# First row block of V computed transposed, with 512 tokens moving past tiles of the weights

## The chip and the metric

The kernel runs on one core of a Trainium2 chip. The metric is device time in microseconds, the median of several runs. The profile is one execution recorded by the hardware profiler; its times are microseconds from the span's start. The engines are PE (TensorE, matmuls; PEld its weight loads), DVE (VectorE), ACT (ScalarE), POOL (GpSimd) and SP (SyncE, which issues nearly all DMAs here).

## The reference

One encoder block on 1024 tokens of width 1024: a joint projection, two groups of attention heads, gates, an output projection and a layer norm.

```python
h = x @ W_in                     # q, k, v, gate of group a; q, k, v, gate of group b
# group a: 8 heads of 64, 2-D neighbourhood attention (8 x 16 window) with a relative bias
# group b: 8 query heads on 2 key/value heads, |i - j| <= 128, rotary positions, a sink logit
p = softmax(q k^T * scale + bias or mask);  o = p v
y = concat(o_a * silu(gate_a), o_b * silu(gate_b)) @ W_out
out = layer_norm(alpha * x + y)
```

The values (V) of both groups are 640 of the columns of `h`: 512 of group a and 128 of group b. The host lays x out transposed (`xT`, columns of x as partitions) and hands the 640 columns apart as `wv`, 1024 x 640.

## The kernel before

The kernel is one function, `hybrid_block`, called by `kernel`. The order of every engine's work is that of the code (`tc.manual_schedule()`, L664), with a list of events that are run at given counts of projection matmuls.

Every product of two f32 matrices is made in three passes from high and low parts: high x high, low x high, high x low. TensorE multiplies a stationary operand of 128 columns, which a weight load brings in, with a moving one.

**Values, first block.** The 1024 tokens are two row blocks of 512. The scales with which x and wv become f16 need the maximum of all x and the sums of wv, so they are not known while the data still arrive. The first block is therefore made in F32R, with parts of x (`xh`, `xl`) and of wv (`wvh`, `wvl`) cast by ACT and subtracted by DVE (POOL for the last two k). First come 26 spins on a small tile (`warm`, L492). `first_tiles` (L528) brings in the first k (128 rows of xT and wv) in halves of 256 tokens and 320 columns; later k's come whole (`load_x`, `load_wv`). `v_mms` (L556) then makes, for each k, four tiles of 128 tokens x two halves of 320 columns x three passes: the stationary operand is 128 tokens of x, the moving one 320 columns of wv, 24 matmuls a k and 192 in all. The sums stand in eight PSUM banks (`tags`, L662).

**Values, second block.** `scales()` (L690) makes `runit` and the like. ACT makes the f16 high parts, DVE the low ones (`x16_part`, `wv_hi`, `wv_lo`), and `v_mms` runs 192 f16 matmuls of 320 columns (L714 on) for the tokens 512 to 1023. Meanwhile `v_out` (L652) copies the first block's banks to `v32[t]`, six by ACT and two by DVE, and `v_max` (L659) takes the maxima of V.

**The projections and what runs beside them.** Then come six projections of 48 f16 matmuls of 512 columns (`project`, L440; the matmul is L459). `at(c, fn)` (L804) hangs a function on matmul c, and these are the ones of this case:

- `v_scale` (L764) at 16: the maximum over the partitions through a transposition on TensorE (L767) and DVE's chain to `vrs`, the reciprocal scale of V.
- the rotary tables cos and sin (`table_load`, L758) at 20.
- `v_part(t)` (L777) at 30 + 8t, one for each of eight token tiles: ACT makes the f16 high part `vt` (L790), DVE the low part (L780) and the copy of group b's part into `vb` (L781), and SP two stores of group a's part to DRAM (`vd`, L783), from where it is fetched row by row later.
- `sum_w(i)` (L793) and `w_scan` take the absolute sums of weight columns on ACT (L799, L270) and DVE (L801). `w_scale(m)` adds them up over the partitions with a tiny matmul on TensorE (L276); DVE's chain L277 to L281 makes the scale `wsc`. With it ACT makes the weights' f16 high part (`wh`, L250) and POOL the low part (`wl`, L255 and L256). A weight buffer (`wr`, L239, two for each projection tile, counted wr0, wr1, ...) is loaded anew when POOL is through with it. In the trace the tiny matmuls of `w_scale(2)` to `w_scale(5)` stand before 68.88, 79.26, 89.65 and 100.03 us, and the last one (`w_scale(NPRO)`) before 106.75.

SP's queue is in order: a DMA whose condition isn't met holds up those behind it. The other engines' queues are in order too.

**Attention.** The unit loop from L1609 on runs heads and row tiles: scores, softmax (`stage_exp`), DMA transposes of the probabilities from `split` to `tr` (L972), products with V (`stage_pv`, L998, which takes `vb` for group b). POOL clears the six `split` tiles beforehand (L857 to L860). The output projection and the norm follow.

Of the kernel before, what the change touches and what calls it, by code (L numbers as in the profile page):

```python
# [7 lines left out]
F32 = mybir.dt.float32  # L8
# [62 lines left out]
def hybrid_block(ctx, tc, xT, x, wt, wv, wo, bias, sink, gain, lbias, cos, sin, bmask, out):  # L71
# [413 lines left out]
    with ExitStack() as vctx:  # L485
# [4 lines left out]
        ps = bank("t")  # L490
        for _ in range(26):
            nc.tensor.matmul(ps[:, :128], warm, warm, start=True, stop=True)  # L492
# [35 lines left out]
        def first_tiles():  # L528
            xr = vp.tile([128, 512], F32, tag="xr", name="xraw", bufs=4)
            wr = wv_stage(0)  # L530
            h = vw.tile([128, 640], F32R, tag="wvh0", name="wvh0")
            l = vw.tile([128, 640], F32R, tag="wvl0", name="wvl0")
            wvh.append(h)
            wvl.append(l)
            for a in (0, 256):
                if a == 0:
                    nc.sync.dma_start(wr[:, :320], wv[0, :, :320])
                nc.sync.dma_start(xr[:, a:a + 256], xT[0, 0, :, a:a + 256])
            nc.sync.dma_start(wr[:, 320:], wv[0, :, 320:])
            xa, xb = xh[0, 0], xl[0, 0]  # L540
            for a in range(2):
                xs, ws = slice(256 * a, 256 * a + 256), slice(320 * a, 320 * a + 320)
                nc.scalar.copy(h[:, ws], wr[:, ws])
                nc.vector.tensor_copy(xa[:, xs], xr[:, xs])
                nc.vector.tensor_sub(xb[:, xs], xr[:, xs], xa[:, xs].bitcast(F32))
                nc.vector.tensor_sub(l[:, ws], wr[:, ws], h[:, ws].bitcast(F32))

# [8 lines left out]
        def v_mms(ps, t, a, k, passes=(0, 1, 2)):  # L556
            ts = slice(128 * (t % 4), 128 * (t % 4) + 128)
            cs = slice(320 * a, 320 * a + 320)
            for i in passes:
                if t < 4:  # L560
                    lh, rh = ((xh[0, k], wvh[k]), (xl[0, k], wvh[k]), (xh[0, k], wvl[k]))[i]
                else:
                    (xa, xb), (wa, wb) = (x16h[1, k], x16l[1, k]), wv16[k]
                    lh, rh = ((xa, wa), (xb, wa), (xa, wb))[i]
                ko = KO if t >= 4 else range(KT)
                nc.tensor.matmul(ps[:, :320], lh[:, ts], rh[:, cs],  # L566
                                 start=(k == ko[0] and i == 0), stop=(k == ko[-1] and i == 2))

# [39 lines left out]
        def wv_hi(k):  # L608
            nc.scalar.activation(wv16[k][0], wraw[k], AF.Copy, scale=wvs)
# [38 lines left out]

        v32 = [vw.tile([128, 640], F32, name=f"v32_{t}") for t in range(8)]
        vm = vw.tile([128, 8], F32, name="vm")  # L650

        def v_out(ps, t, a, eng="act"):  # L652
            cs = slice(320 * a, 320 * a + 320)
            if t >= 4:
                nc.scalar.activation(v32[t][:, cs], ps[:, :320], AF.Copy, scale=vdq)
            else:
                (nc.scalar.copy if eng == "act" else nc.vector.tensor_copy)(v32[t][:, cs], ps[:, :320])

        def v_max(t):  # L659
            nc.vector.tensor_reduce(vm[:, t:t + 1], v32[t], axis=AXX, op=ALU.max, apply_absolute_value=True)  # L660

        tags = ("pj", "pj", "s", "s", "t", "t", "s", "s")  # L662
        banks = [bank(t) for t in tags]
        ordered.enter_context(tc.manual_schedule())  # L664
        first_tiles()
        interleave(load_x(0, 1), load_wv(1))
        for k in range(KT):
# [12 lines left out]
            if k < 5 or k == 6:  # L680
                interleave(*gens)
            for a in range(2):
# [20 lines left out]

        wv_hi(KO[0])
        x16_part(1, KO[0])
        for i, eng in ((0, "act"), (2, "act"), (6, "dve"), (1, "dve"), (3, "act"), (7, "act")):
            v_out(banks[i], i // 2, i % 2, eng)
        wv_lo(KO[0])
        ahead(1)
        v_out(banks[4], 2, 0)  # L710
        ahead(2)
        v_out(banks[5], 2, 1)
        nc.vector.tensor_mul(vdq, unit[:, 0:1], unit[:, 1:2])
# [8 lines left out]
        for i, k in enumerate(KO):  # L722
# [10 lines left out]
            if i in (4, 6):  # L733
                w_scale(i // 2 - 2)
            if i >= 4:
                v_max(i - 4)
        for t in (0, 1, 3):
# [3 lines left out]
        for a in range(2):  # L741
            ps = bank(tags[4 + a])
            for k in KO:
                v_mms(ps, 6, a, k)
            if a == 0:
                x16_part(0, 1)
                w_split(0)
                x16_part(0, 2)
                v_max(4)
            else:  # L750
                x16_part(0, 3)
                v_max(5)
                v_max(7)
                w_split(1)
            v_out(ps, 6, a)
        v_max(6)

# [19 lines left out]
        def v_part(t):  # L777
            if t > 0:
                vt, v3 = vts.pop(t - 1)
                nc.vector.scalar_tensor_tensor(vt[:, :, 1, :HD], v3, vrs, vt[:, :, 0, :HD], op0=ALU.mult, op1=ALU.subtract)  # L780
                nc.vector.tensor_copy(vb[:, t - 1], vt[:, 8:10, :, :HD])  # L781
                for i in range(2):
                    nc.sync.dma_start(  # L783
                        vd[:, :, 2 * (t - 1) + i, :].rearrange("q c e -> c q e"),
                        vt[GW * i:GW * i + GW, 0:8].rearrange("p (q h) i e -> p q (h i e)", h=2))
            if t < 8:
                vt = vp.tile([128, 10, 2, VE], F16, tag=("vt", "wvr")[t % 2], name=f"vt{t}", bufs=3)
                v3 = v32[t].rearrange("p (h e) -> p h e", e=HD)
                nc.gpsimd.memset(vt[:, 0:8, :, HD:VE], 1.0 / PSCALE)
                nc.scalar.activation(vt[:, :, 0, :HD], v3, AF.Copy, scale=vrs)  # L790
                vts[t] = vt, v3

# [186 lines left out]
    def stage_pv(q):  # L979
        ps = st[q, "o"] = bank("t")  # L980
        for m in range(4):
# [6 lines left out]
            for i in range(c):  # L988
# [4 lines left out]
                else:  # L993
                    v = [vb[d, k, p // 2, e, :] for e in range(2)]
                ph, pl = tr[d, i, :], tr[d, c + i, :]
# [788 lines left out]
```

## Time and profile before

| | |
|---|---|
| median of 3 runs | 432.82 us (432.66 to 433.52) |
| the profiled execution | 433.62 us, span 431.7 us, granted clock 0.999 |
| spins | 0.99 to 3.94 us |
| first k of the values; second k on | 3.87 to 8.6 us; from 8.64 us |
| f16 block of the values | from 33.39 us |
| projections | from 59.70 us |
| PE busy in each ten us from 10 to 130 | 10.00 |

The first half of a row of the page names the line, the engine, the operation and the tiles written and read; then come count, busy time and mean length of one, and the idle time of the engine just before, with what ended it. Matmuls overlap, so the pitch of a row of them is read from their starts, not from their lengths.

### The profile page before, as it was taken

The page shows a single profiled execution, that of the slowest core. Times are in us where ns is not written, and L with a number is a line of the kernel's source. Part 1 is how long each engine was busy: PE and PEld are TensorE (multiplying, and loading weights), DVE is VectorE, ACT ScalarE, POOL GpSimd, SP SyncE. Part 2 cuts the span into 40 slices and gives each one's busy share as a digit, 9 for nine tenths or more (in the row PEclk, how much of TensorE's full clock was granted, in tenths as well). Part 3 has the DMA queues.
Part 4 walks back from the last instruction along what each step waited for, and adds up shares of the span by engine and source line. Part 5 has one row for each costly group of instructions (what it writes and reads, how often), then busy time and mean ns, then how long its engine had stood idle before and what let it go on. Part 6 is the DMA issues. An engine that isn't in the chain of part 4 may idle for free.

```text
span 431.7 us, 9375 instructions
## 1 busy us (share of the span) xinstructions
PE 425.5 (99%) x3175; PEld 249.1 (58%) x3175; DVE 343.5 (80%) x856; ACT 317.8 (74%) x682; POOL 291.4 (67%) x300
## 2 busy tenths in 40 slices
PE   8999999999999999999999999999999999999995
PEld 7997764444445555656555655555565655444444
DVE  4978966884887888888789897897887875597685
ACT  4759789888659989778998866889878883653313
POOL 0030075789468867788999977668889799649354
PEclk9999999999999999999999999999999999999999
DMA  7947768992448999989799999997999989942222
GB/s 249 392 167 241 240 197 291 278 318 55 140 135 173 192 167 219 197 157 154 146 225 229 199 171 187 246 178 125 237 194 200 187 169 234 402 172 97 99 98 99
DMA packets 131552, 84.81 MB, mean 196 GB/s; under 512 B 97584, under 2 KB 106928, under 8 KB 131504
## 3 DMA queue, kind: packets, MB, share of 16 engines
q1 hardware_dynamic: 131360, 84.08, 81.6%
q8 instruction: 25, 0.41, 0.4%
q14 instruction: 23, 0.19, 0.2%
q10 hardware_dynamic: 144, 0.13, 0.1%
HBM read 50.60 MB, written 10.52 MB: 142 GB/s over the span
## 4 chain that ended last, share of the span: by engine, by line
PE 94%; DMA 2%; POOL 1%; ACT 0%; SPq 0%; DVE 0%; issue 0%; POOLq 0%; ACTq 0%
PE ps_pj L459 50%; PE ps_t L998 7%; PE ps_s L1310 7%; PE ps_s L566 6%; PE ps_pj L1310 5%; PE ps_t L1310 4%; PE ps_s L921 4%; PE ps_s L922 4%; PE ps_pj L566 3%; PE ps_t L566 3%; PE ps_t L1035 2%; DMA wvraw<-in_wv 1%; DMA tr<-split 1%; POOL xr L1455 0%; POOL xr L1458 0%
## 5 line engine op out<-in xcount | busy, mean ns | idle before, releaser
L459 PE MATMUL ps_pj<-xf,wh 128*128 128x512 f16 x672 | 201.3, 379 | 0.0
L459 PE MATMUL ps_pj<-xf,wl 128*128 128x512 f16 x336 | 127.3, 379 | 0.0
L459 PEld LDWEIGHTS <-wh 128*128 128x128 f16 x672 | 63.7, 98 | 58.3
L951 ACT ACTIVATE ps_s<-sn,nm 128x321 f32<-128x321 f32 (+3 forms) x128 | 67.8, 529 | 32.0 <-DVE nm L935 30.4
L970 DVE SCALAR_TENSOR_TENSOR split<-ps_s,split 128x320 f16<-128x320 f32 (+2 forms) x128 | 62.6, 489 | 18.4 <-ACT split L969 16.8
L255 POOL TENSOR_SCALAR wr<-wr,wsc 128x512 f32<-128x512 f32 x32 | 23.9, 746 | 55.9 <-ACT wh L250 51.3
L969 ACT ACTIVATE split<-ps_s 128x320 f16<-128x320 f32 (+2 forms) x128 | 55.1, 430 | 3.1 <-DMA tr<-split 1.3
L459 PEld LDWEIGHTS <-wl 128*128 128x128 f16 x336 | 32.8, 98 | 37.9
L935 DVE CUSTOM_DVE_ANT_0 sn<-ps_s,bm,nsk 128x320 f32<-128x320 f32 (+2 forms) x64 | 37.0, 579 | 8.9 <-PE ps_s L922 8.7
L256 POOL TENSOR_TENSOR wl<-wr,wh 128x512 f16<-128x512 f32 x32 | 39.6, 1238 | 2.7
L935 DVE CUSTOM_DVE_ANT_0 sn<-ps_s,bias,sg 128x368 f32<-128x368 f32 (+1 forms) x64 | 36.1, 564 | 3.7 <-PE ps_s L922 3.3
L921 PE MATMUL ps_s<-ks,qs 128*128 128x320 f16 (+3 forms) x128 | 38.2, 298 | 0.0
L922 PE MATMUL ps_s<-ks,qs 128*128 128x320 f16 (+3 forms) x128 | 38.2, 298 | 0.0
L998 PEld LDWEIGHTS <-tr 128*128 128x128 f16 (+1 forms) x1056 | 36.3, 98 | 2.3 <-DMA tr<-split 0.4
L369 POOL COPY ks<-ks 64x512 f16<-64x512 f16 x40 | 25.9, 647 | 8.4 <-ACT ks L313 6.0
L1310 PEld LDWEIGHTS <-m 128*128 128x128 f16 x186 | 17.8, 98 | 19.3 <-POOL m L1231 0.2
L1455 POOL TENSOR_TENSOR xr<-xr,gb 128x512 f32<-128x512 f32 (+1 forms) x11 | 12.3, 1123 | 18.3 <-ACT xr L1439 18.3
L250 ACT ACTIVATE wh<-wr,wsc 128x512 f16<-128x512 f32 x32 | 22.7, 710 | 0.9 <-DVE wsc L280 0.9
L566 PEld LDWEIGHTS <-xf 128*128 128x128 f16 x192 | 18.6, 98 | 7.3
L921 PEld LDWEIGHTS <-qs 128*128 128x128 f16 x128 | 12.5, 98 | 15.1
L922 PEld LDWEIGHTS <-qs 128*128 128x128 f16 x128 | 12.5, 98 | 15.0
L998 PE MATMUL ps_t<-va,tr 128*128 128x65 f16 (+1 forms) x528 | 19.1, 193 | 0.0
(269 smaller groups left out, 933.1 us busy)
## 6 DMA issues: line engine op xcount, KB each, us to landing
wr<-in_wt SPq DMA_DIRECT2D x32, 256.0 KB, 3.3
ws<-in_wt SPq DMA_DIRECT2D x15, 512.0 KB, 6.3
wor<-in_wo SPq DMA_DIRECT2D x20, 256.0 KB, 4.1
xr<-in_x SPq DMA_DIRECT2D x8, 512.0 KB, 9.7
out<-xr SPq DMA_DIRECT2D x14, 256.0 KB, 2.0
bias<-in_bias SPq DMA_DIRECT2D x8, 440.0 KB, 4.3
wob<-in_wo SPq DMA_DIRECT2D x12, 256.0 KB, 4.2
wvraw<-in_wv SPq DMA_DIRECT2D x9, 320.0 KB, 6.4
```

Source lines behind the costliest of these rows:

```text
L256: nc.gpsimd.tensor_sub(l, raw, h)
L369: nc.gpsimd.tensor_copy(place(t, o, half, col), place(t, a, half, col))
L459: nc.tensor.matmul(ps, a[:, k % 4, :], mv, start=(k == 0 and i == 0), stop=(k == KT - 1 and i == 2))
L566: nc.tensor.matmul(ps[:, :320], lh[:, ts], rh[:, cs], start=(k == ko[0] and i == 0), stop=(k == ko[-1] and i == 2))
L921: nc.tensor.matmul(ps[:, :n], q, sl[0], start=True, stop=False)
L922: nc.tensor.matmul(ps[:, :n], q, sl[1], start=False, stop=True)
L935: nc.vector.tensor_tensor_reduce(sn[:, at0:at0 + n], ps[:, :n], bias_t, sg[:, c:c + 1], init, op0=ALU.add, op1=ALU.min, accum_out=nm)
L951: nc.scalar.activation(pt[:, c], sn[:, c], AF.Exp, bias=nm, scale=-1.0, accum_out=acc)
L969: nc.scalar.activation(h, pt[:, c], AF.Copy, scale=PSCALE)
L970: nc.vector.scalar_tensor_tensor(l, pt[:, c], PSCALE, h, op0=ALU.mult, op1=ALU.subtract)
L998: nc.tensor.matmul(ps[:, w * m:w * m + e], a, b_, start=(i == 0), stop=(i == len(mms) - 1))
L1310: nc.tensor.matmul(ps[:, cs], lh[:, 128 * t:128 * t + 128], rh[:, cs], start=(fresh and e == 0 and n == 0), stop=(e == len(terms) - 1 and ...
```

## The change

The first block of V is made transposed: the stationary operand is now a tile of 128 columns of wv (five of them, `j`), the moving one all 512 tokens of x. `vt_mm` (L570 of the changed kernel) makes 15 matmuls of 512 columns a k, 120 in all, two of which are made in halves of 256; five banks hold the sums. The first k goes in an order of its own, k = 1 to 6 pass by pass, the last k bank by bank. Eight spins go, and two matmuls of 512 columns on `warm` (L671) clear the two banks into which halves are added. `first_tiles` cuts wv into 256 and 384 columns, and ACT casts the second half of x.

On PE, this is what stands where the second k of the first block begins (bank<-operands, columns). Before:

```order
L566 MATMUL ps_pj<-wvh_214,x_79 128x320
L566 MATMUL ps_s<-wvh_214,x_79 128x320
L566 MATMUL ps_t<-wvh_214,x_79 128x320
L566 MATMUL ps_s<-wvh_214,x_79 128x320
L566 MATMUL ps_pj<-wvh_214,x_79 128x320
L566 MATMUL ps_s<-wvh_214,x_79 128x320
```

And now, the whole of that k:

```order
L570 MATMUL ps_s<-x_79,wvh_206 128x512 x3
L570 MATMUL ps_t<-x_79,wvh_206 128x512 x2
L570 MATMUL ps_s<-x_79,wvh_206 128x512 x3
L570 MATMUL ps_t<-x_79,wvh_206 128x512 x2
L570 MATMUL ps_s<-x_79,wvl_207 128x512 x3
L570 MATMUL ps_t<-x_79,wvl_207 128x512 x2
```

The six rows before are a quarter of a k; the six now are all 15 matmuls of one.

The evacuation is five copies of 512 columns (`vt_out`, L662; DVE for j = 0, 1, 3, ACT for 2 and 4), and the maxima are taken of five tiles of 512 and four of 640. `v_scale` is hung on step 10, cos on 10 and sin on 12.

V of the first block must then be turned. For each j, `vt_part` (ACT, high part) and `vt_part2` (DVE, low part) fill `vhl`; `vt_turn` (L825) is a DMA transpose of eight blocks of 128 x 128, f16, for j = 4 straight into `vb`, for the others into `vtd`; `vt_store` (L830, L832) copies these on DVE into `vtt` with the columns of ones and stores them to `vd`. The token tiles 4 to 7 keep their way in `v_part` and `v_part2`. Each step hangs on 26 + 6.4 (n + step). The layout of `vb` changes with it, and `stage_pv` reads it accordingly.

This is SP's queue about the rotary tables. Before (`wr` weight loads, `ws` loads for the weight sums, `vd` the stores):

```order
L239 DMA wr_891<-in_wt 128x512
L239 DMA wr_912<-in_wt 128x512
L720 DMA ws_917<-in_wt 128x2x512
L760 DMA cos<-in_cos 128x1024
L760 DMA sin<-in_sin 128x1024
L720 DMA ws_952<-in_wt 128x2x512
L783 DMA vd<-vt_957 64x4x260 x2
L720 DMA ws_980<-in_wt 128x2x512
L783 DMA vd<-vt_972 64x4x260 x2
L239 DMA wr_1008<-in_wt 128x512
```

Now:

```order
L239 DMA wr_811<-in_wt 128x512
L776 DMA cos<-in_cos 128x1024
L776 DMA sin<-in_sin 128x1024
L239 DMA wr_845<-in_wt 128x512
L736 DMA ws_850<-in_wt 128x2x512
L736 DMA ws_874<-in_wt 128x2x512
L825 DMA_TRANSPOSE vb<-vhl_869 128x8x128
L736 DMA ws_903<-in_wt 128x2x512
L825 DMA_TRANSPOSE vtd_915<-vhl_882 128x8x128
L239 DMA wr_931<-in_wt 128x512
L825 DMA_TRANSPOSE vtd_937<-vhl_894 128x8x128
```

The tables stand one weight load and one `ws` load earlier, and transposes stand where stores stood; the stores follow later.

And this is DVE's queue ahead of the chain of `w_scale(3)` (`wg`). Before:

```order
L801 TENSOR_REDUCE wm<-ws_694 128x1
L780 SCALAR_TENSOR_TENSOR vt_1063<-v_5_179,vrs,vt_1063 128x10x64
L781 COPY vb<-vt_1063 128x256
L780 SCALAR_TENSOR_TENSOR vt_1086<-v_6_180,vrs,vt_1086 128x10x64
L781 COPY vb<-vt_1086 128x256
L277 TENSOR_REDUCE wg<-ps_t 128x1
```

Now:

```order
L842 TENSOR_REDUCE wm<-ws_614 128x1
L830 COPY vtt_884<-vtd_915 128x8x64 x2
L800 SCALAR_TENSOR_TENSOR vt_994<-v_6_168,vrs,vt_994 128x10x64
L801 COPY vb<-vt_994 128x256
L830 COPY vtt_896<-vtd_937 128x8x64 x2
L800 SCALAR_TENSOR_TENSOR vt_1020<-v_7_169,vrs,vt_1020 128x10x64
L801 COPY vb<-vt_1020 128x256
L830 COPY vtt_920<-vtd_954 128x8x64 x2
L277 TENSOR_REDUCE wg<-ps_t 128x1
```

The last token tile now comes ahead of the chain, and three pairs of copies that read the transposes' results stand there too.

The clearing of the `split` tiles goes from POOL to DVE, on the steps 200 to 230. The core of the diff:

```diff
-    vb = zp.tile([128, 8, 2, 2, HD], F16, tag="zv", name="vb", bufs=1)
+    vb = zp.tile([128, 8, 2, 128], F16, tag="zv", name="vb", bufs=1)
...
-        for _ in range(26):
+        for _ in range(18):
             nc.tensor.matmul(ps[:, :128], warm, warm, start=True, stop=True)
...
+        def vt_mm(j, k, i, s=slice(0, 512)):
+            h, l, x0, xd = wvh[k], wvl[k], xh[0, k], xl[0, k]
+            lh, rh = ((h, x0), (h, xd), (l, x0))[i]
+            nc.tensor.matmul(banks[j][:, s], lh[:, 128 * j:128 * j + 128], rh[:, s],
+                             start=(k == 0 and i == 0 and j > 1), stop=(k == KT - 1 and i == 2), skip_group_check=True)
...
-        banks = [bank(t) for t in tags]
+        banks = [bank(t) for t in ("s", "s", "s", "t", "t")]
+        for j in range(2):
+            nc.tensor.matmul(banks[j].rearrange("p (a c) -> p a c", c=128), warm, warm.unsqueeze(1).to_broadcast([128, 4, 128]),
+                             start=True, stop=False, skip_group_check=True)
...
-            for a in range(2):
-                for ts in ((0, 1), (2, 3)) if k == 0 else ((0, 1, 2, 3),) if k < KT - 1 else ((0,), (1,), (3,), (2,)):
-                    for ps in (0,), (1,), (2,):
-                        for t in ts:
-                            v_mms(banks[2 * t + a], t, a, k, ps)
+            if k == 0:
+                for s in (slice(0, 256), slice(256, 512)):
+                    for j in range(2):
+                        vt_mm(j, 0, 0, s)
+                order = [(j, i) for i in (1, 2) for j in range(2)] + [(j, i) for i in range(3) for j in range(2, 5)]
+            elif k < KT - 1:
+                order = [(j, i) for i in range(3) for j in range(5)]
+            else:
+                order = [(j, i) for j in range(5) for i in range(3)]
+            for j, i in order:
+                vt_mm(j, k, i)
...
+        def vt_turn(j):
+            hl = vts.pop(("hl", j)).rearrange("p t i c -> p (t i c)")
+            if j == 4:
+                to = vb[:, :4]
+            else:
+                to = vts["td", j] = vw.tile([128, 4, 2, 128], F16, tag=("wvl0", "wvl1", "wvl2", "wvl0")[j], name=f"vtd{j}")
+            nc.sync.dma_start(to.rearrange("p t i c -> p (t i) c"), hl, transpose=True)
+
+        def vt_store(j):
+            td, vt = vts.pop(("td", j)), vts.pop(("vt", j))
+            for i in range(2):
+                nc.vector.tensor_copy(vt[:, :, :, i, :HD], td[:, :, i].rearrange("p t (h e) -> p t h e", e=HD))
+            for i in range(2):
+                nc.sync.dma_start(vd[j, :, i:8:2, :], vt[GW * i:GW * i + GW].rearrange("p t h i e -> p t (h i e)"))
...
-        at(16, v_scale)
-        at(20, table_load, "cos", cos, "zc")
-        at(20, table_load, "sin", sin, "zs")
-        for t in range(9):
-            at(30 + 8 * t, v_part, t)
+        at(10, v_scale)
+        at(10, table_load, "cos", cos, "zc")
+        at(12, table_load, "sin", sin, "zs")
+        for n, (kind, j) in enumerate((("j", 4), ("j", 0), ("j", 1), ("j", 2), ("j", 3), ("t", 4), ("t", 5), ("t", 6), ("t", 7))):
+            for step, fn in ((0, vt_part), (1, vt_part2), (2, vt_turn), (7, vt_store)) if kind == "j" else ((0, v_part), (1, v_part2)):
+                if (fn, j) != (vt_store, 4):
+                    at(26 + int(6.4 * (n + step)), fn, j)
...
-    for t in split:
-        nc.gpsimd.memset(t, 0.0)
+    for i, t in enumerate(split):
+        at(200 + 6 * i, nc.vector.memset, t, 0.0)
```

More of the change, by code (lines that the diff above doesn't have):

```diff
@@ L559, in v_mms @@
             for i in passes:
[L560 to L567, printed above, removed]
+                (xa, xb), (wa, wb) = (x16h[1, k], x16l[1, k]), wv16[k]
+                lh, rh = ((xa, wa), (xb, wa), (xa, wb))[i]
+                nc.tensor.matmul(ps[:, :320], lh[:, ts], rh[:, cs],
+                                 start=(k == KO[0] and i == 0), stop=(k == KO[-1] and i == 2))
+        def vt_mm(j, k, i, s=slice(0, 512)):
[3 more added lines that the diff above has]
+                             start=(k == 0 and i == 0 and j > 1), stop=(k == KT - 1 and i == 2), skip_group_check=True)
         AXX = mybir.AxisListType.X
@@ L734, in hybrid_block @@
                 w_scale(i // 2 - 2)
-            if i >= 4:
-                v_max(i - 4)
+            if i >= 3:
+                v_max(i - 3)
         for t in (0, 1, 3):
@@ L777, in v_part @@
         def v_part(t):
[L778 to L785, printed above, removed]
@@ L993, in stage_pv @@
                 else:
-                    v = [vb[d, k, p // 2, e, :] for e in range(2)]
+                    v = [vb[d, k, e, HD * (p // 2):HD * (p // 2) + HD] for e in range(2)]
                 ph, pl = tr[d, i, :], tr[d, c + i, :]
```

89 lines of the change are left out of this document (54 added, 35 removed).

## The prediction

> **What bounds the kernel now.** The page comes first: how busy TensorE is, and what the chain that ended last is made of.
>
> ```profile
> PE 425.5 (99%) x3175; PEld 249.1 (58%) x3175; DVE 343.5 (80%) x856; ACT 317.8 (74%) x682; POOL 291.4 (67%) x300
> PE 94%; DMA 2%; POOL 1%; ACT 0%; SPq 0%; DVE 0%; issue 0%; POOLq 0%; ACTq 0%
> ```
>
> TensorE is the bound nearly throughout, so what counts is the pitch of its matmuls and any new hole between them. The chain of waits over the edited stretch gives the pitches (start, length, what, how many).
>
> ```profile
> 8.64 0.41 PE ps_pj L566
> 32.23 0.88 PE ps_s L566 x6
> 53.18 6.52 PE ps_t L566 x48
> 89.65 10.38 PE ps_pj L459 x48
> 100.03 6.71 PE ps_pj L459 x31
> ```
>
> From 8.64 us on nothing but matmuls stands in it. Three pitches: the first values block (F32R, 320 columns) 0.88/6 = 0.1467 us; the second block (f16, 320 columns) 6.52/48 = 0.1358; a projection (f16, 512 columns) 10.38/48 = 0.2163. Per column the first costs 0.458 ns, the others 0.424 and 0.422. The timeline of the matmuls and of the weight loads (PEld) shows what is odd about the first.
>
> ```profile
> 28.11 0.31 PE L566 MATMUL ps_pj<-wvh,x 128*128 128x320 f32 x1
> 33.39 0.31 PE L566 MATMUL ps_pj<-wq,xf 128*128 128x320 f16 x1
> 28.11 0.19 PEld L566 LDWEIGHTS ps_s<-wvh,x 128*128 128x128 f32 x1
> L459 PEld LDWEIGHTS <-wh 128*128 128x128 f16 x672 | 63.7, 98 | 58.3
> ```
>
> An f32 load takes 0.19 us and starts with the matmul ahead of it; an f16 load takes 0.098. A 320-column stream lasts 0.136, less than the f32 load. I read it so: at 320 columns the F32R block goes at the pace of its loads.
>
> **The first block.** 192 matmuls of 320 columns become 120 of 512 (two of them in halves): 61,440 columns both times, but 120 loads. A 512-column stream of 0.2163 covers a load of 0.19, so I take 0.2163. Counted from 8.64, where the second k begins, 7 k of 15 matmuls take 105 x 0.2163 = 22.71, and the f16 block starts at 31.35 instead of 33.39: **2.04 us gained**. The bounds: were the excess 0.1467 - 0.1358 = 0.011 a fixed cost of every F32R matmul, the pitch would be 0.2272 and the gain 0.89; were it a cost per column, the pitch would be 0.2347 and the gain 0.1. The Trainium skill, page "TensorE: Matmul & The Clock Gate", section "Back-to-back issue gap", speaks against the change: its isolated gap is N/2.4 + 2.5 ns whatever the type, 135.8 at 320 and 215.8 at 512, by which the old block would already cost what its columns cost and 0.1 us could be gained. The f16 rows agree with it (0.1358, 0.2163); the F32R row does not (0.1467).
>
> The first k hardly counts, for the second waits for data. Spins, first matmul and casts (start, length):
>
> ```profile
> L492 PE MATMUL ps_t<-warm 128*128 128x128 f16 x26 | 3.0, 313 | 1.0 <-DVE warm L140 1.0
> 3.87 0.60 PE L566 MATMUL ps_pj<-wvh,x 128*128 128x320 f32 x1
> 4.80 0.29 DVE L544 CAST x<-xraw 128x256 fp32r<-128x256 f32 x1 [0.21 <-DMA xraw<-in_xT]
> 7.87 0.72 ACT L522 CAST wvh<-wvraw 128x640 fp32r<-128x640 f32 x1 [1.36 <-DMA wvraw<-in_wv]
> ```
>
> ACT waits for wv's second slice until 7.87, and the order of the casts ahead of it doesn't alter that. The second half of x comes at 4.80; cast by ACT it is ready near 5.2, and the 3.2 us of the first k (15 x 0.2163) begun there end near 8.5, before 8.64. The eight spins taken out (8/26 of 3.0 us, 0.9) make room for two clearing matmuls of four times the columns, the same time: cost nothing. But until 5.2 only two halves can run, so TensorE pauses; if its pace fell back there (the first matmul after the spins took 0.60, later ones 0.31), up to 1 us of the first k would be late.
>
> The f16 block must be ready at 31.35:
>
> ```profile
> 29.10 0.17 DVE L599 RECIPROCAL runit<-unit 128x2 f32<-128x2 f32 x1
> 30.04 0.71 ACT L629 ACTIVATE xf<-x,runit 128x512 f16<-128x512 f32 x1
> 30.78 0.75 DVE L630 SCALAR_TENSOR_TENSOR xf<-x,runit,xf 128x512 f16<-128x512 f32 x1 [1.51 <-ACT xf L629]
> L657 DVE COPY v<-ps_s 128x320 f32<-128x320 f32 x1 | 0.5, 482 | 0.0
> 63.30 0.29 DVE L768 TENSOR_REDUCE vg<-ps_s 128x1 f32<-128x128 f32 x1 [1.98 <-PE ps_s L767]
> ```
>
> Its scales are known at 29.27 as before, its first operands at 30.75; x's low half follows at 31.53 and is wanted after six matmuls, at 32.17. DVE's two 512-column evacuations in between (about 0.66 each, from 0.48 for 320 columns) fit its idle 1.51. Cost nothing, with 0.6 in hand; were that cover gone, TensorE would stand for what is missing. The other three evacuations, the maxima and the high and low halves keep their number of columns and lie beside TensorE's work. v_scale goes from step 16 to step 10, past nothing that waits: DVE idled 1.98 for TensorE's transposition there, so its chain to `vrs` now starts near 60 instead of at 63.30.
>
> **The projection stage.** SP now issues cos and sin behind an earlier weight load, and five DMA transposes among the loads. The share of busy DMA time (last column but one) and SP's rows:
>
> ```profile
> core 0: us, PE busy (x) PEld busy (x) DVE busy (x) ACT busy (x) POOL busy (x), PEclk, DMA share, GB/s
> 10.00:20.00 10.00, 10.00 (x70) 10.00 (x69) 9.91 (x17) 7.97 (x16) 0.00 (x0) 1.00 1.05 394
> 66.00:68.00 2.00, 2.00 (x11) 0.88 (x10) 0.93 (x1) 2.00 (x5) 1.57 (x5) 1.00 0.75 231
> 70.00:80.00 10.00, 10.00 (x49) 4.54 (x48) 8.42 (x11) 9.57 (x17) 7.81 (x9) 1.00 1.07 328
> 94.00:96.00 2.00, 2.00 (x11) 0.90 (x10) 1.97 (x2) 1.86 (x5) 1.88 (x3) 1.00 0.88 323
> 62.93 0.33 SPq L239 DMA_DIRECT2D wr<-in_wt  x1
> 65.69 0.38 SPq L720 DMA_DIRECT2D ws<-in_wt  x1
> 66.17 0.41 SPq L760 DMA_DIRECT2D cos<-in_cos  x1
> L972 SPq DMA_TRANSPOSE tr<-split x128: 1188/1217/2417, 127.1 to 357.9; - x128
> SPq L239 <- POOL wl L256: 18.2, 6, 6.7
> ```
>
> From 67 to 95 the DMA engines have a backlog. SP itself waited 18.2 us for POOL (the queue's own waits, the last row), so the issue time of five more DMAs, 5 x 1.22 = 6.1, finds room; the number of `vd` stores stays 16. But the transfers lengthen the backlog. Who waits for its end? The twelfth weight load, wr11, is scanned by ACT, and the weight sum on TensorE (w_scale(5)) needs that scan:
>
> ```profile
> 97.28 0.19 ACT L270 ACTIVATION_READ_ACCUMULATOR junk<-wr 128x1 f32 x1
> 99.86 0.17 PE L276 MATMUL ps_t<-wm,ones 128*128 128x2 bf16 x1
> 101.38 0.69 ACT L420 ACTIVATE z<-ps_pj,inv 128x512 f32<-128x512 f32 x1 [0.41 <-PE ps_pj L459]
> 104.71 0.19 ACT L799 ACTIVATION_READ_ACCUMULATOR junk<-ws 128x1 f32 x1
> ```
>
> Now the scan is done at 97.47 and the sum runs at 99.86. Afterwards the sum comes at 97.82. The scan: the backlog begins with cos right behind the load of row 62.93, 2.04 earlier, at 61.3; ws8, its old head, was issued 0.5 ahead of cos at 65.7; so it begins 4.4 earlier. The five transposes add 256 KB each: at the 394 GB/s of row 10:20 that is 0.67, at the issue time of a transpose 1.22; I take 0.96, 4.8 in all (3.3 to 6.1). The Trainium skill, page "DMA: Bandwidth & Descriptors", section "Latency and other measured facts", has 261 GB/s for strided transposes; by it the five would take 5.0. SP also stands still twice (behind POOL's low half for the tenth load, behind DVE's first `vtt` copies for the fifth transpose), letting the backlog run dry: 0.8, from 0 to 2. So the scan ends at 97.47 - 4.4 + 4.8 + 0.8 = 98.67 (96.4 to 101.2) and TensorE stands 0.85 (0 to 3.4). The last sum, at 106.57 before and so at 106.57 - 2.04 + 0.85 = 105.4, follows ACT's scan of row 104.71, which ended 7.4 after wr11's with 0.4 of it waiting for TensorE; 7.0 after 98.67 is 105.7, so up to 0.3 more, of which I take 0.15. **Sum: -2.04 + 1.0 = -1.04 us.** Everything behind keeps its order and moves along. ACT's cast of ks now waits for the last two `vd` stores of the values; they stand some nine transfers ahead of wr11 in the backlog, so ACT, which has the cast queued ahead of wr11's scan, is through with it first. The six `split` memsets move from POOL to DVE behind the last sum, where no one on TensorE's path waits for them.
>
> **The rivals.**
> Nothing late (A'): the transposes take 3.3 or the DMA engines never run dry; the whole 2.04 stays, 430.8.
> Fixed cost per F32R matmul (B): 0.89 gained at first, so the sum comes at 98.97, later than the scan; 431.9. Cost per column (C), where the change does not do what it says: 432.7. The f16 pitches, equal per column at 320 and 512, speak against both. A late clock in the first k costs up to 1 us: 432 at best.
> Slower (D): DVE's queue. Before w_scale(3)'s group (row 81.50 below) now stand three pairs of `vtt` copies, each pair behind a transpose.
>
> ```profile
> 74.56 1.53 ACT L790 ACTIVATE vt<-v,vrs 128x640 f16<-128x640 f32 x2
> 73.27 1.17 DVE L781 COPY vb<-vt 128x256 f16<-128x256 f16 x1
> 81.35 0.23 DVE L781 COPY vb<-vt 128x256 f16<-128x256 f16 x1
> 81.50 0.15 DVE L277 TENSOR_REDUCE wg<-ps_t 128x1 f32<-128x2 f32 x1
> 86.81 0.19 ACT L270 ACTIVATION_READ_ACCUMULATOR junk<-wr 128x1 f32 x1
> 83.07 0.69 POOL L255 TENSOR_SCALAR wr<-wr,wsc 128x512 f32<-128x512 f32 x1 [2.45 <-ACT wh L250]
> ```
>
> A copy takes 0.23 alone and 1.17 while POOL works. With vt5's high half out near 74.05 (76.09 - 2.04), three subtractions of 0.89, a reduction of 1.21 and nine copies of c follow: the group is reached at 77.9 + 9c. The scan for the next sum ends 5.5 after it (81.50, 87.00), and that sum comes at 89.65 - 0.2 - 2.04 = 87.4; so it costs from c = 0.44 on. I take 0.4, since POOL idles 2.45 there. At 0.66 the loss is 2.0 and the gain is gone; at 0.85 it is 3.7: 1.7 slower, 434.5.
>
> **How the numbers follow.** The profiled execution took 433.62 (span 431.7 and 1.92 around it), 0.80 over the median of 432.82. With -1.04 it would be 432.6, and the median 431.8. Chances: the forecast 0.44 (its own range 430.9 to 432.9), A' 0.24, B 0.08, C 0.05, the clock 0.04, D 0.15. 0.2%, 0.87 us, is about what a measurement of this kernel can tell from no change. Faster: A' and three fifths of the forecast, a little of B, 0.54; slower: nearly all of D, 0.15; the rest, 0.31, within. The range, 430.6 to 433.4, takes in A', B and C and leaves out D's upper part.
>
> **What would show it.** Right: F32R matmuls of 512 columns 0.216 apart; the f16 block starting near 31.4; w_scale(5)'s sum standing about 0.9 behind ACT's scan of wr11. Wrong: a pitch of 0.227 or more; no hole near 98 (A'); a hole near 87 behind the scan of the tenth load (D). A second k that starts later than 8.7 would mean that the new first k is not covered.

## The result and the profile after

The changed kernel takes 438.58 us (median of 6 runs, 437.21 to 439.71); the kernel before took 433.17 in the same comparison (6 runs, 432.19 to 435.93). The ratio is 1.012, 95% interval 1.0097 to 1.0142: **slower by 5.4 us**, where 431.8 (430.6 to 433.4) was forecast. The profiled execution took 439.15 us, its span is 437.4. The page's row of busy times and its chain that ended last:

```profile
PE 426.3 (97%) x3099; PEld 243.3 (56%) x3099; DVE 346.6 (79%) x868; ACT 316.8 (72%) x680; POOL 285.8 (65%) x294
PE 76%; POOL 7%; DMA 5%; DVE 4%; issue 3%; ACT 1%; SPq 1%; POOLq 0%; ACTq 0%
```

76 matmuls fewer, yet PE's busy time is 0.8 longer, and PE's part of the chain fell from 94% to 76%. From about 60 to 103 us the chain now runs through other engines and DMAs. Pieces of it (start, length, what):

```profile
28.64 2.04 PE ps_s L570 x9
30.68 1.36 PE ps_t L570 x6
...
81.23 3.09 DMA vd<-vt
84.38 1.15 POOL wl L256
89.42 5.63 DMA vd<-vt
95.87 0.91 POOL ks L369
96.78 5.58 DMA wr<-in_wt
103.38 8.40 PE ps_pj L459 x31
```

The first two rows give the F32R pitch at 512 columns: 3.40/15 = 0.2267 us. Then the chain goes through stores of `vd` to the load of wr11 (96.78), and behind that a piece of 31 projection matmuls takes 8.40 us where it took 6.71. The timeline of PE at the three places (a number in square brackets is the time for which the engine stood idle just before, with what it waited for; such a stretch on PE is called a hole below):

```profile
31.88 0.31 PE L564 MATMUL ps_pj<-wq,xf 128*128 128x320 f16 x1
...
103.22 0.16 PE L276 MATMUL ps_t<-wm,ones 128*128 128x2 bf16 x1 [4.70 <-ACT junk L270]
103.99 1.06 PE L459 MATMUL ps_pj<-xf,wh 128*128 128x512 f16 x2
104.84 0.63 PE L459 MATMUL ps_pj<-xf,wl 128*128 128x512 f16 x1
105.27 1.06 PE L459 MATMUL ps_pj<-xf,wh 128*128 128x512 f16 x2
...
111.62 0.17 PE L276 MATMUL ps_t<-wm,ones 128*128 128x15 bf16 x1
```

The f16 block starts at 31.88 instead of 33.39: **1.51 gained**. The sum of w_scale(5) stands at 103.22 instead of 99.86, so the hole cost 4.87 from there (its row says 4.70 of waiting). From 103.99 to 105.27 three matmuls take 1.28, or 0.427 each, nearly twice the 0.2163, and from 104 to 107 us the granted clock reads 0.50; this lasts until 107.3, and the last sum, 6.72 behind that of w_scale(5) before, is 8.40 behind it: 1.68 lost to a slow stretch behind the hole. -1.51 + 4.87 + 1.68 = 5.04. The attention gives 0.6 back, at gaps that stand between 165 and 178 us in the trace of the kernel before, and the output stage loses 1.5, of which more below.

Why the scan came late stands on ACT's timeline and on that of SP's queue (where the second column runs from the first issue of a row to the end of its last, waits in between included). ACT:

```profile
95.12 1.26 ACT L315 CAST ks<-rp 64x512 f16<-64x512 f32 x2 [3.86 <-DMA vd<-vt]
98.83 0.67 ACT L420 ACTIVATE z<-ps_pj,inv 128x512 f32<-128x512 f32 x1
102.45 0.63 ACT L270 ACTIVATE junk<-wr 128x512 bf16<-128x512 f32 x1 [2.95 <-DMA wr<-in_wt]
```

And SP:

```profile
68.71 3.32 SPq L825 DMA_TRANSPOSE vtd<-vhl  x1
76.36 0.50 SPq L239 DMA_DIRECT2D wr<-in_wt  x1
79.16 1.23 SPq L825 DMA_TRANSPOSE vtd<-vhl  x1
92.20 3.04 SPq L651 DMA_DIRECT2D tf<-wot  x4
95.33 1.29 SPq L832 DMA_DIRECT2D vd<-vtt  x2
96.78 0.50 SPq L239 DMA_DIRECT2D wr<-in_wt  x1
```

Two waits stand on ACT: first the cast of ks for the last value stores, then, 2.95 us, the load itself. SP issued that load at 96.78 (before: 90.26), behind the tables' stores and the last pair of `vtt`. The DMA engines meanwhile, in stretches of 5 us (last columns: PE's granted clock, the DMA engines' share and GB/s), in the kernel before:

```profile
80.00:85.00 5.00, 5.00 (x25) 1.00 1.11 275
85.00:90.00 5.00, 5.00 (x26) 1.00 1.06 323
90.00:95.00 5.00, 5.00 (x25) 1.00 1.06 306
95.00:100.00 5.00, 5.00 (x26) 1.00 0.32 119
```

And in the changed one:

```profile
80.00:85.00 5.00, 5.00 (x25) 1.00 0.77 161
85.00:90.00 5.00, 5.00 (x26) 1.00 0.93 253
90.00:95.00 5.00, 5.00 (x25) 1.00 1.02 195
95.00:100.00 5.00, 3.52 (x17) 1.00 1.10 328
100.00:105.00 5.00, 1.78 (x7) 0.88 0.95 328
105.00:110.00 5.00, 5.00 (x20) 0.78 0.02 7
```

Counted against a share of 1.00, they idle 0.23 x 5 + 0.07 x 5 = 1.5 us from 80 to 90, after SP had stood from 76.86 to 79.16. From 90 to 95, where 884 of 1206 packets have between 512 and 2048 bytes, as the 520-byte pieces of the `vd` stores have (512 of 1226 before), a full share moves 195 GB/s instead of 306. The backlog, the transfers that stand one behind another at the DMA engines, ended at 95 before and now ends past 102. Over the whole of it, from 61.3 to 95.1 us before and to 102.4 now, the mean share is nearly the same (0.96 and 0.97) at 281 and 261 GB/s: on the whole the engines weren't idler, they moved some 1.2 MB more, and at a lower rate.

### The profile page after: what moved, and what is told of

It reads as the page before. It is cut to its first block, busy times and chain, and to the rows that moved or that the text cites. A ratio compares the mean times of both kernels' runs of the same rounds, so it can differ in the third digit from the quotient of the medians.

```text
span 437.4 us, 9230 instructions
## 1 busy us (share of the span) xinstructions
PE 426.3 (97%) x3099; PEld 243.3 (56%) x3099; DVE 346.6 (79%) x868; ACT 316.8 (72%) x680; POOL 285.8 (65%) x294
## 4 chain that ended last, share of the span: by engine, by line
PE 76%; POOL 7%; DMA 5%; DVE 4%; issue 3%; ACT 1%; SPq 1%; POOLq 0%; ACTq 0%
PE ps_pj L459 39%; PE ps_t L1041 6%; PE ps_s L1353 4%; PE ps_s L570 4%; PE ps_s L964 4%; PE ps_s L965 4%; PE ps_pj L1353 3%; PE ps_s L564 3%; PE ps_t L1353 3%; PE ps_t L570 2%; DMA vd<-vt 2%; DMA xr<-in_x 2%; PE ps_pj L564 2%; PE ps_t L564 1%; DMA wr<-in_wt 1%
```

## The experiments

Each kernel is the changed one with the edits shown, but for e11. In the table: when SP issued wr11 and when ACT began its scan, PE's wait at w_scale(5), all from the one profiled execution, and the median of all runs with the ratio to the kernel before on the same chip. In the profiles of e4 and e12 all of PE's work runs some 2.7 us later than in the changed kernel's, from the first k on (see the last section), and these moments are later with it.

| kernel | wr11 issued | scan | wait | median | ratio (95%) |
|---|---|---|---|---|---|
| changed | 96.78 | 102.45 | 4.7 | 438.58 | 1.012 (1.0097 to 1.0142) |
| e1_tables_last | 95.40 | 100.33 | 2.6 | 437.09 | 1.010 (1.0047 to 1.0154) |
| e2_own_buffer | 96.74 | 101.67 | 3.7 | 438.49 | 1.0113 (1.0071 to 1.0155) |
| e3_both | 94.53 | 99.34 | 1.1 | 434.01 | 1.0015 (0.9999 to 1.0031) |
| e4_no_turning | 97.25 | 102.01 | 1.6 | 435.28 | 1.0037 (1.0013 to 1.006) |
| e5_tags | 94.83 | 100.15 | 1.9 | 436.18 | 1.006 (1.0042 to 1.0078) |
| e6_store_later | 94.18 | 100.21 | 1.7 | 433.58 | 1.0014 (0.999 to 1.0038) |
| e7_tags_store | 95.13 | 99.51 | 1.1 | 432.65 | 0.9995 (0.9976 to 1.0014) |
| e9_stores_last | 87.62 | 95.72 | 0 | 432.36 | 0.9967 (0.9944 to 0.9989) |
| e10_all_stores_last | 85.54 | 95.49 | 0 | 431.84 | 0.9958 (0.9938 to 0.9979) |
| e12_order_alone | 92.72 | 102.10 | 1.7 | 434.31 | 1.0016 (1.0 to 1.0031) |

Three theories: Q, the order on SP's queue keeps wr11 back; X, the transposes' transfer time does; A, ACT's cast of ks does, which waits for the last value stores.

**e1_tables_last: the tables' stores behind wr11.**

```diff
-        at(90, t_store)
+        at(99, t_store)
```

> The changed kernel with the four stores of wot (t_store) put on step 99 instead of 90, so that SP issues wr11's load and ws14's ahead of them; nothing else. Theory Q (the queue: SP hands wr11's load out late, because all 16 value stores, the four wot stores and a held fifth transpose stand ahead of it): wr11 issued near 93.3 instead of 96.8, lands near 99, the hole at w_scale(5) falls from 4.9 us to about 1.4 and the slow clock after it mostly goes; 433.5 to 434.5 us. Theory X (the transfers: the five transposes' own time on the DMA engines delays all behind them): about the same here, since 3.5 us of transfers leave wr11's way. Theory A (ACT: its cast of ks waits for the last value stores, and the scan stands behind it): no gain over 0.5 us, 438.

The wait fell from 4.7 to 2.6 us, and the scan came 2.1 earlier, though wr11 was issued only 1.4 earlier. That speaks against A alone (no gain over 0.5); Q and X had been given the same numbers here, so this run doesn't part them. The 4 runs lie between 434.05, the profiled one, and 439.61, so the median says little.

**e2_own_buffer: the fourth turned tile doesn't wait for the first.**

```diff
-tag=("wvl0", "wvl1", "wvl2", "wvl0")[j], name=f"vtd{j}")
+tag=("wvl0", "wvl1", "wvl2", "vt32_0")[j], name=f"vtd{j}")
```

> The changed kernel with a buffer of its own for the fifth transpose (that of vt32_0, which has long been read), so that it no longer waits for DVE's copies out of the first; nothing else. Theory Q: the fifth transpose is issued near 76.9 instead of 79.2, all behind it 2.3 earlier; the hole falls to about 2.6, 435 to 436 us. Theory X: the DMA engines have as much to move, they were idle for at most 1.5 us in 80 to 90; the hole falls by at most 1.5, 437 to 438. Theory A: as Q, since the last stores move too.

The fifth transpose no longer stands behind DVE's copies: it is issued at 77.19. But SP then stood 1.9 us for earlier stores to land, and wr11 went out no earlier (96.74). The wait is 1.0 shorter, within X's bound of 1.5 and short of Q's 2.3; the time is the same, which none of the three had: in the profile the slow stretch behind the wait was longer and took 2.6 us instead of 1.7.

**e3_both: both edits.**

> Both edits together: own buffer for the fifth transpose, and the wot stores on step 99. Theory Q: wr11 lands 5.5 to 6 earlier than in the changed kernel, before 97.5, no hole; the time is that of the kernel before less the 1.5 us that TensorE gained in the first block, 431.5 to 432. Theory X: a hole of 1 us or more stays, 433 or more. Theory A: a hole near 1 us stays unless the last value stores land before 93; 432.5.

The wait is 1.1 us, less than the two gains one by one would leave (4.7 - 2.1 - 1.0 = 1.6), and 4.6 us of the time are gone, the slow stretch among them. Q had been given no wait and 431.5 to 432, and that did not come; the numbers are those of X (a wait of 1 us or more, 433 or more), and A's wait near 1 us fits too.

**e4_no_turning: DVE copies the untransposed tiles instead of the DMA transposes.** The first block's values stay unturned.

```diff
...
-                to = vts["td", j] = vw.tile([128, 4, 2, 128], F16, ...
-            nc.sync.dma_start(to.rearrange("p t i c -> p (t i) c"), hl, transpose=True)
+                vts["td", j] = vts["hl", j]
```

> The changed kernel without the five DMA transposes: group b's values of the first block are copied unturned by DVE into vb and group a's are stored unturned, so the first block's values are wrong. All else, the 16 stores, the wot stores and their order, stays. Theories Q and X: wr11 lands before 97.5, no hole, 431.5 to 432 us. If a hole of over 1 us stays, it is not the transposes but the stores that come in one run, or ACT's wait for them (theory A).

Without any transpose 1.6 us of waiting are left, and 3.3 us of the time are gone. So X alone isn't it: the stores' order on SP is the same, and from 75 to 85 the DMA engines were idle for four tenths (shares 0.46 and 0.73). No wait had been forecast by Q either. What was set down beforehand for a wait that stays, the stores that come in one run, fits: ACT idled 1.87 us for wr11. What the transposes' own time costs and what they cost by holding SP up, this kernel can't tell apart.

**e5_tags: e3_both, and the cast of ks waits for tile 5's stores alone.**

```diff
-            vt = vts[t] = vp.tile(..., tag=("vt", "wvr")[t % 2], ...
+            vt = vts[t] = vp.tile(..., tag=("wvr", "wvr", "vt", "vt")[t - 4], ...
```

> The kernel with the fourth turned tile in a buffer of its own and the table stores last (e3_both) still had a hole of 1.1 us at w_scale(5). There ACT's cast of ks stood until 94.94, when the last value stores landed, so that ACT was through with what stands ahead of wr11's scan at 99.31; wr11 itself landed at 99.25. This kernel adds one edit: the stored tiles of tokens 4 and 5 share one set of buffers and those of 6 and 7 the other, so that the cast waits for tile 5's stores alone. If the cast is the cause (A), the hole closes and the kernel gains about 1 us over e3_both: 432.9 us by the medians (434.0 less 1.1). If wr11's place on SP is the cause (Q), the scan still starts at wr11's landing, 99.3, the hole stays at 1.0 to 1.1 us and the time at 434.0. The two waits end within 0.1 us of each other, so I expect Q's numbers here, with ACT idle just ahead of the scan.

As expected, the hole stayed. ACT now stands idle for 4.05 us ahead of the scan, waiting for wr11 and nothing else:

```profile
95.44 0.67 ACT L420 ACTIVATE z<-ps_pj,inv 128x512 f32<-128x512 f32 x1
100.15 0.63 ACT L270 ACTIVATE junk<-wr 128x512 bf16<-128x512 f32 x1 [4.05 <-DMA wr<-in_wt]
```

That the median is 2.2 over e3's I had not expected (0.5 of it may lie with the chip: the kernel before took 433.58 there and 433.12 beside e3). In the profile the wait was 1.9, and the matmuls behind it went at half their pace for some 3.6 us, which cost 1.7 more (its last sum comes 8.40 after that of w_scale(5), as in the changed kernel).

**e6_store_later: e3_both, and the fourth turned tile's stores behind wr11.**

```diff
-                    at(26 + int(6.4 * (n + step)), fn, j)
+                    at(101 if (fn, j) == (vt_store, 3) else 26 + int(6.4 * (n + step)), fn, j)
```

> e3_both with one other edit: the two stores of the fourth turned tile are made behind the tables' stores (step 101), so that SP issues wr11 before them. wr11's issue should come from 94.5 to about 92, its landing from 99.25 to about 97. By Q the hole closes: 432.9 us. By A the cast of ks still stands until about 94.9 and ACT is through at 99.3, so the hole stays at 1.0 to 1.1 us: 434.0 us. Since both waits end at the same time in e3_both, I expect A's numbers here: one of the two alone gives nothing.

The time is e3's (ratios 1.0014 and 1.0015), the wait 1.7. ACT began the cast at 95.94, after 3.85 us of waiting for the stores, and reached the scan at 100.21 without idling: A's account, as expected. But wr11 itself was issued at 94.18 and not at 92, so the edit hardly moved what it was meant to move.

**e7_tags_store: both of these.**

> Both edits of e5_tags and e6_store_later. If the hole of e3_both has these two causes side by side, it goes only here: no wait at w_scale(5), or under 0.3 us, and a median of 432.7 us (434.0 less 1.1 less the 0.2 at the last sum), 0.4 us under the kernel before and 1.3 us under e3_both. If the hole stays at 1 us a third thing holds wr11's scan.

The median came out as expected, the reason not, so that is luck: the wait of 1.1 us is still there. SP waited 2.7 us, up to 92.57, for earlier stores to land before it could issue the next load, so wr11 went out no earlier (95.13), and ACT idled 3.18 ahead of its scan. A third thing was left, and it was the queue again.

**e8_halves: the changed kernel's 512-column matmuls as two of 256** (from the second k on).

```diff
-                vt_mm(j, k, i)
+                for s in (slice(0, 512),) if k == 0 else (slice(0, 256), slice(256, 512)):
+                    vt_mm(j, k, i, s)
```

> The changed kernel with each 512-column matmul of the first block made as two of 256 columns with the same weights, from the second k on (210 matmuls instead of 105). It tells what the pitch of an F32R matmul is made of. With a fixed 0.0105 us on each, a 256-column one takes 256/512 of (0.2267 - 0.0105) plus 0.0105, or 0.1186 us, and the block is 1.1 us longer. If the pace of the weight loads sets the floor, as I held in the prediction, it stands at 0.147 us, the pitch at 320 columns, and the block is 7 us longer. If it is a price per column, it takes 0.1134 us and the block is no longer.

```profile
20.80 0.88 PE L570 MATMUL ps_s<-x,wvh 128*128 128x256 f32 x6
21.52 0.64 PE L570 MATMUL ps_t<-x,wvh 128*128 128x256 f32 x4
22.00 0.88 PE L570 MATMUL ps_s<-x,wvl 128*128 128x256 f32 x6
```

Ten matmuls from 20.80 to 22.00: 0.1200 us each. With 0.1467 at 320 and 0.2267 at 512 columns this is a straight line, 0.1067/256 = 0.417 ns a column and 0.0133 us on every matmul, whatever its columns. The loads set no floor: each of these matmuls has a weight load of its own in the trace, 0.19 us long, and one follows the other every 0.1200 us all the same. (One run, 440.71 us.)

**e9_stores_last: e7, with the second and third turned tile's stores behind wr11 too.**

```diff
+                    at(101 if fn == vt_store and j > 0 else 26 + int(6.4 * (n + step)), fn, j)
```

> e7_tags_store with the stores of the second and third turned tile, too, behind the tables' stores (step 101), so that of the turned tiles' stores only the first pair goes before wr11. In e7 wr11 was issued at 95.13 and landed at 99.42, ACT idle for 3.2 us ahead of its scan: the queue alone was left as the cause. Four stores fewer stand ahead of wr11; in e7 SP issued them from 86.53 to 94.47, with a hold of 2.7 us on earlier stores' landing. If the order on SP is the cause, wr11 is issued by 92.5 and lands by 97.8, under the 98.3 at which its scan must begin, the hole at w_scale(5) is under 0.3 us, and the median is 431.5 us, 1.1 under e7 and some 2 us under the kernel before. If the transposes' share of the DMA engines is the cause, whatever the order, the landing stays past 99 and the hole at about 1 us: 432.6 us.

The hole is gone. SP's queue:

```profile
86.60 0.56 SPq L736 DMA_DIRECT2D ws<-in_wt  x1
87.62 0.59 SPq L239 DMA_DIRECT2D wr<-in_wt  x1
89.13 0.37 SPq L736 DMA_DIRECT2D ws<-in_wt  x1
91.58 2.61 SPq L651 DMA_DIRECT2D tf<-wot  x4
94.28 5.16 SPq L832 DMA_DIRECT2D vd<-vtt  x6
```

And PE at the sum:

```profile
98.21 0.38 PE L459 MATMUL ps_pj<-xf,wl 128*128 128x512 f16 x1
98.42 0.17 PE L276 MATMUL ps_t<-wm,ones 128*128 128x2 bf16 x1
```

wr11 is issued before the tables' four stores and the six of the turned tiles; the sum stands at 98.42, 1.44 before that of the kernel before, without a wait. The transposes are all still there. The kernel is faster than the one before by 0.33% (0.11 to 0.56). The median is 0.9 above the 431.5 that the order had been given and 0.2 under the 432.6 of the transposes' share, and e7's interval overlaps with this one: the times alone wouldn't part the two accounts. That it is the order stands on the trace, on wr11's landing before its scan at 95.72 and the sum without a wait.

**e10_all_stores_last: the first turned tile's stores too** (`fn == vt_store` alone).

> e9_stores_last with the first turned tile's stores behind the tables' too. Two stores fewer again ahead of wr11; if e9 has closed the hole this does nothing more (431.5 us), if e9 left some of it this takes up to the rest. What could be lost is the far end: eight stores then start at about 97 to 104, and the loads behind them (wr12 and on) land later than the 106 of e7; if one of these is late, a hole of up to 2 us opens past 110.

431.84 us (431.09 to 433.1), 0.42% under the kernel before (0.21 to 0.62): the best version here. From e9 it can't be told apart, and the loads behind the stores were not late.

**e11_hole_alone: the kernel before with a hole put in.**

```diff
+                    for _ in range(7 if n == 3 else 0):
+                        nc.scalar.activation(junk[:, :1024], junk[:, :1024], AF.Abs)
                     w_scan(2 * n + 5)
```

> The kernel before, with nothing of the change: ahead of wr11's scan, ACT makes seven activations of 128x1024 into a tile nobody reads. Each takes 1.06 us, 7.4 in all, and the scan, which ended at 97.47, had 2.3 us to spare up to w_scale(5)'s sum at 99.86: a hole of 5 us should open there, as long as the changed kernel's 4.7 to 4.9. It tells what such a hole costs by itself. If the hole costs only its length, less 0.6 us that the gaps at 165 to 178 give back: 433.4 + 5.0 - 0.6, or 437.8 us. If PE's clock falls to half for about 3.4 us behind it, as in the changed kernel's profile, 1.7 more: 439.5 us. Then the changed kernel's 438.5 is this hole and this clock less the 1.5 us that its first block gains, and nothing else need be sought.

440.41 us (439.81 to 441.18), ratio 1.0154 (1.0125 to 1.0183): 7.1 over the kernel before, 0.9 more than I counted with.

```profile
105.19 0.16 PE L276 MATMUL ps_t<-wm,ones 128*128 128x2 bf16 x1 [5.12 <-ACT junk L270]
106.45 1.06 PE L461 MATMUL ps_pj<-xf,wh 128*128 128x512 f16 x2
107.30 0.63 PE L461 MATMUL ps_pj<-xf,wl 128*128 128x512 f16 x1
107.73 1.06 PE L461 MATMUL ps_pj<-xf,wh 128*128 128x512 f16 x2
```

The sum is 5.33 late, and again the matmuls behind it stand 1.28/3 = 0.427 apart; until the pace is back 1.9 more is lost. So a hole of this length has this price without anything of the change. In the profile the output stage loses 0.8 besides, which I had not counted.

**e12_order_alone: the changed kernel with the order of e9's stores, but the shared buffers.** (`at(99, t_store)` and e9's line.)

> The changed kernel with its order of stores alone altered: the tables' stores at step 99 and those of the second to fourth turned tile at 101, as in e9_stores_last. The fourth turned tile keeps the first one's buffer, and the stored tiles their two sets of buffers, so that ACT's cast of ks again waits for tile 7's stores. If the order of the stores is the whole cause, the hole at w_scale(5) is under 0.5 us and the median that of e9, 432.4 us. If the shared buffer counts as it did between e1_tables_last and e3_both (1.5 us of the hole), wr11 is issued some 1.5 us later than e9's 87.6, and its landing at about 97 is still in time; the cast, which ended at 94.9 to 96 where it waited for tile 7's stores, would let the scan begin at 98 to 99.5, so that up to 1 us of hole stays: 432.4 to 433.5 us. Over 434 us neither holds.

The median is 434.31, over the 434 past which neither account was to hold; how much of that is the late first k, which the profiled run shows, is not known. The second account's mechanism is what the profile shows. The cast of ks waited 4.48 us:

```profile
97.83 1.26 ACT L315 CAST ks<-rp 64x512 f16<-64x512 f32 x2 [4.48 <-DMA vd<-vt]
101.53 0.67 ACT L420 ACTIVATE z<-ps_pj,inv 128x512 f32<-128x512 f32 x1
102.10 0.62 ACT L270 ACTIVATE junk<-wr 128x512 bf16<-128x512 f32 x1
```

ACT reached wr11's scan at 102.10 without idling for the load (if the late start of PE made it late by as much, 2.7 us, that is 99.4, within the expected 98 to 99.5). Here A is the wait that ends last: once the order of the stores is right, the buffer for which the cast waits decides. Queue order, the shared turned tile and the cast's buffer are three waits side by side. In the two kernels in which the hole closes (e9, e10) all three are taken away, and the order alone leaves 1.7 us; whether the turned tile's own buffer is still needed once the order and the cast are right was not run.

## Why the prediction was wrong

**The first block (a gain of 2.04).** The sign was right, the reason for its size wrong. I read 0.1467 at 320 columns as the pace of the weight loads, which 512 columns would hide; e8 shows a fixed 0.0133 us on every F32R matmul, so that one of 512 columns takes 0.0104 longer than an f16 one (0.2267 against 0.2163). That is rival B: 105 x 0.2267 = 23.80 against 22.71, 1.1 us of the gain gone. In the profile 1.51 was gained all the same, by luck as far as the sum goes, since the second k began at 7.91 and not at 8.64; e9 and e10 gained 1.44 and 1.27. The Trainium skill, page "TensorE: Matmul & The Clock Gate", section "Back-to-back issue gap", has a fixed part, but of 2.5 ns, and names no type ("whatever the type" was my reading); f16 agrees here, F32R (13.3 ns) does not.

**The first k.** That data would let the second k begin at 8.64 whatever the casts do was read from one run's landing of wv: the starts of the f16 block were 31.86 to 32.60 in nine profiles of kernels with the changed first block (0.8 to 1.5 under the 33.39 before) and 34.5 in two (e4, e12).

**The scan of wr11 (98.67, range 96.4 to 101.2).** This is the step that failed: it ended at 103.2, 4.5 late, past the upper bound. I named the right load, queue and sum, but made one stream of bytes of it: time saved at the head plus five transfers plus 0.8 for SP's stands. Three things were missing. SP's queue is an order: with the fifth transpose held up to 79.16, every store and then wr11 came later, and the DMA engines idled 1.5 us from 80 to 90 and not 0.8. In the stretch of 90 to 95, full of the small pieces of the stores bunched ahead of wr11, a full share moved 195 GB/s, which the 394 or 306 of other stretches don't price. And one more weight load, 256 KB, stood within the backlog than I counted: the one behind cos and sin. e9 shows that the bytes alone don't make the hole: the same transfers, in another order and with three tiles in other buffers, leave none. How the 4.5 us split among the three was not measured.

**ACT's cast of ks.** "Through with it first" was wrong: the stores for which it waits landed so late (95.1) that the scan couldn't have begun before about 99.5. In the changed kernel the later landing of wr11 hid this; in e6 and e12 it was what ended last.

**What the hole costs.** I priced it at its length. Behind the hole of 4.7 us the granted clock read 0.50 for some 3 us and the matmuls went at half their pace, which cost 1.68 more; e11 shows the same apart from the change (1.9 more behind 5.1 us). The prediction had no such term. The Trainium skill, page "TensorE: Matmul & The Clock Gate", section "What's actually happening", has it: half clock after an idle window of about 3.4 us, full clock again after a busy one, the windows running free. The clock of 0.50 and the 0.427 us agree, and the stretch of 3.6 us (103.7 to 107.3) too. By it e5's hole of 1.9 us would be too short, and yet 3.6 us at half pace followed: there the measurement decides.

**Rival D** did not come. DVE reached w_scale(3)'s group at 81.97; the three pairs of copies took 1.67, 0.49 and 0.49, and PE did not wait there. The f16 block, v_scale and the memsets cost nothing, as said.

**The sum** with what was measured: -1.51 + 4.87 + 1.68 - 0.6 + 1.5 = 5.9 up to the last matmul of the output projection, where the forecast had -2.04 + 0.85 + 0.15. The spans of the two profiles differ by 5.7, the medians by 5.4. The 1.5 in the output stage doesn't hang on the hole: e10, without a hole, loses 1.45 at the same place in its profile, e9 nothing, and e11, without the change, 0.8. PE waits there for DVE's `xr` (L1386), 0.9 us in the changed kernel and 1.3 in e10; why in one run and not in another stays open.

## What to carry to other kernels

A queue that issues in order is to be read as an order, not as a stream of bytes: ask what stands ahead of the one load that a tight consumer needs, and move work that nobody waits for (here the stores) behind it, before counting bandwidth. Where several waits end close together, taking one away shows the next; list them all, with the time at which each ends. A hole on TensorE of some microseconds costs its length and can cost a stretch at half pace besides (here 1.7 to 2.6 us behind holes of 1.9 to 5.1), so its price jumps.

## What the runs showed of the hardware

- A hole of 1.9 us (e5) was followed by a stretch at half pace, one of 2.6 us (e1) was not, holes of 3.7, 4.7 and 5.1 us were, and none of 1.1 to 1.7 (e3, e4, e6, e7, e12). So between 1.9 and 2.6 us length alone doesn't decide it. The same kernel can go either way, it seems: e1's profiled run has a mean granted clock of 0.998, its three others 0.990 to 0.994; how long their holes were is not on record. In all runs of the changed kernel, e2 and e11 it is 0.990 to 0.996; in the 79 runs of the kernel before beside the experiments it is 0.997 to 1.000, but for one of 0.995.
- The first k is exposed as well. In e12's profile the first slice of x came 1 us later, PE waited 0.92 for its cast, and the matmuls of the first k began 0.43 apart instead of 0.227, though the granted clock reads 1.00 throughout:

```profile
4.86 2.04 PE L570 MATMUL ps_s<-x,wvh 128*128 128x256 f32 x6 [0.92 <-DVE x L542]
6.70 1.05 PE L570 MATMUL ps_s<-x,wvl 128*128 128x512 f32 x2
7.56 0.63 PE L570 MATMUL ps_s<-x,wvh 128*128 128x512 f32 x1
7.98 1.05 PE L570 MATMUL ps_t<-x,wvh 128*128 128x512 f32 x2
```

The f16 block then began at 34.54, 2.7 us later than in the changed kernel's profile. In e4's profile it was the same (a wait of 1.08, the block at 34.53). I had given this 1 us and a chance of 0.04; how often it comes, and whether the kernel before has it, one profile of each can't say.
